# A weight's high and low part written separately, and every instruction held to the planner's order

## The chip, the cores and the metric

The kernel runs on one core of one Trainium2 chip. What counts is the device time of one execution in microseconds (us): the median over several runs. One execution was also recorded by the hardware profiler, and all rows quoted below come from such recordings. The engines are named as in the profile: PE (TensorE, the matrix engine; PEld is its weight load), DVE (VectorE), ACT (ScalarE), POOL (GpSimd) and SP (SyncE, which here only issues transfers).

## The reference, cut to what matters

A decoder trunk of two layers on 256 tokens of 1024 features, all in float32. Each layer has three sub-layers, each with an RMS norm before and after it:

```python
for l in range(DEPTH):
    f = swiglu(rms_norm(x, ffn1_pre_g[l]), ffn1_w_gu[l], ffn1_w_down[l])
    x = x + 0.5 * rms_norm(f, ffn1_post_g[l])
    m = hybrid_mixer(rms_norm(x, mix_pre_g[l]), mix_w_in[l], mix_w_out[l], ...)
    x = x + rms_norm(m, mix_post_g[l])
    f = swiglu(rms_norm(x, ffn2_pre_g[l]), ffn2_w_gu[l], ffn2_w_down[l])
    x = x + 0.5 * rms_norm(f, ffn2_post_g[l])
```

`swiglu` is `silu(x @ gate) * (x @ up)` (2816 wide) times `w_down`. The mixer projects to 2566 columns, runs three heads side by side (a gated linear recurrence, a state-space block in chunks, a gated product over chunks of 128 tokens) and projects back. The weights are 170 MB and each is read once.

## The kernel before, in words

**Matmuls in three parts.** PE multiplies in a rounded format (float32r). To keep float32 precision each operand is split into a high part (a rounded copy) and a low part (what the rounding left), and a product is the sum of three: high x high, high x low, low x high. For a weight, ACT makes the high part (line 406, or line 410 when a norm's gain is multiplied in) and DVE the low part from the original and the high part (line 407 or 411). So each low part waits for its high part on another engine. The normalised input nT is split in the same way: ACT casts the transposed tile, DVE subtracts (both through the helper at line 137).

**Weights.** `weight_units` lists 656 units of 128 rows by up to 512 columns in the order of their use. `weight_chunks` packs them four to a transfer (the first five transfers hold 1, 1, 2, 2 and 2). SP loads a chunk into one of three staging tiles (`dma_chunk`, line 355); the split parts go into one of 17 weight slots, or in some phases into scratch tiles. `fill` (line 374) splits as many units ahead as slots allow.

**Three matmul loops.** In the first block of a feed-forward layer and the first part of the mixer the 128 tokens of each half t are the stationary operand (`a_step`, `mm3`, line 435). In the other feed-forward blocks the weight is stationary, and the high and low part of all 256 tokens pass in one matmul of 512 columns, then one of 256 (`wide_tile`, line 741). The mixer's other columns use `b_tile` (line 718). The product with `w_down` again uses `mm3`: it finishes token half 0 first and has the last four or five steps of half 1 run while half 0 is normalised (`down`, `post`, `pre`).

**Side work.** All that isn't a main matmul is written as a Python generator, a `Chain`: `post` (square sums on ACT, a power on POOL, the update of x on DVE), `pre` (transposes of x on PE, the split into nT, square sums, the power `rs` on POOL, its spread by PE into `rb`), `evac_block` (silu, the product with up, transposes on PE, the split), and the mixer's heads.

**What sets the order.** The kernel carries a model of its own: `self.T` holds a clock for each engine and for transfers, and each operation adds its cost in us (a 512-column matmul 512 x 0.000417 = 0.2135; a high part 0.095 + 512 x 0.000833, and 0.095 more with a gain; a POOL power 0.47). PE's clock is "now". `Chain.op` (line 129) writes an operation when now comes within 0.7 us of the time at which its inputs are ready (PE: not before they are ready; an operation that follows one on its own engine: 2 us). `fill` writes a weight's split when a slot is free, its transfer is modelled as landed and the clocks of DVE and ACT are at most 0.6 us (FILL) ahead of now; the high and the low part are then written one right behind the other (`split_next`, line 393).

**What holds that order.** `keep` (line 294) pins an instruction behind the one written before it on its engine, but only while now is below PIN, 15 modelled us, or when asked for one operation. What is not pinned may be put elsewhere in its engine's queue by the compiler's scheduler, by estimates of its own, as far as data allow. Each engine has one list of instructions, called its queue below.

Of the kernel before, what the change touches and what calls it, by code (L numbers as in the profile page):

```python
# [8 lines left out]
F32 = mybir.dt.float32  # L9
# [3 lines left out]
ALU = mybir.AluOpType  # L13
PSUM = bass.MemoryType.PSUM

P = 128
# [12 lines left out]
HOP = 0.13  # L29
# [4 lines left out]
EXTRA_MIX = (2, 4)  # L34
NF = 3
FIRST = 0
PIN = 15.0

C_GATE, C_REC, C_Z, C_XBC, C_DT, C_UV = 0, 384, 768, 1152, 2048, 2054
XS0, B0, C0 = C_XBC, C_XBC + 384, C_XBC + 640  # L40
# [10 lines left out]
def weight_units():  # L51
    units = []

    def add(name, l, blocks, scale=None):
        units.append((name, l, blocks, scale))

    def ffn(l, w):
        gu, dn, pg = f"ffn{w}_w_gu", f"ffn{w}_w_down", f"ffn{w}"
        for b in range(5):
            for off in (0, DFF):  # L60
                for k in range(KT):
                    add(gu, l, [(k * P, off + b * 512, 512)], (pg, k))
        for k in range(KT):
            add(gu, l, [(k * P, 2560, 256), (k * P, DFF + 2560, 256)], (pg, k))
        for k in range(DKT):
            for n in range(2):
                add(dn, l, [(k * P, n * 512, 512)])

    for l in range(DEPTH):
        ffn(l, 1)  # L70
        for k in range(KT):
            add("mix_w_in", l, [(k * P, C_DT, 6), (k * P, C_Z, 384)], ("mix", k))
        for k in range(KT):
            add("mix_w_in", l, [(k * P, C_UV, 512)], ("mix", k))
        for grp in FGROUPS:
            for k in range(KT):
                add("mix_w_in", l, [(k * P, c, P) for _, _, c in grp], ("mix", k))
        for k in OUT_KTS:
            for n in range(2):
                add("mix_w_out", l, [(k * P, n * 512, 512)], ("norm", k - 3) if 3 <= k < 6 else None)  # L80
        ffn(l, 2)
    return units


def weight_chunks(units):
    chunks, i = [], 0
    head = [1, 1, 2, 2, 2]
    while i < len(units):
        n = head.pop(0) if head else CHUNK
        chunks.append(list(range(i, min(i + n, len(units)))))  # L90
        i += n
    return chunks


def unit_width(u):
    return sum(w for _, _, w in u[2])
# [13 lines left out]
class Chain:  # L110


    def __init__(self, k, t=None):
        self.k = k
        self.t = k.T["pe"] if t is None else t
        self.eng = None
        self.pin = False
# [104 lines left out]
class Kernel:  # L222
    def __init__(self, ctx, tc, x, wts, pf, pb, gpost, wst, wri, out):
        self.tc, self.nc = tc, tc.nc
        self.x_d, self.w_d, self.pf_d, self.pb_d = x, wts, pf, pb
        self.gp_d, self.wst_d, self.wri_d, self.out_d = gpost, wst, wri, out
        mk = lambda n, **k: ctx.enter_context(tc.tile_pool(name=n, **k))
        self.cp = mk("cp", bufs=1)
        self.lp = mk("lp", bufs=1)
        self.sp = mk("sp", bufs=8)  # L230
        self.stg = mk("stg", bufs=NSTG)
        self.scr = mk("scr", bufs=1)
        self.tp = mk("tp", bufs=1)
        self.acc = mk("acc", bufs=1, space=PSUM)
        self.free_slots = {"a": [f"a{i}" for i in range(NSCR)], "m": [f"m{i}" for i in range(8)],
                           "w": [f"w{i}" for i in range(NSLOT)], "f": [f"f{i}" for i in range(NF)]}
        self.banks = [(f"acc{i}", 0.0) for i in range(8)]
        self.side_banks = 0
        self.T = {"pe": 0.0, "act": 0.0, "dve": 0.0, "pool": 0.0, "dma": 2.0}
        self.table = self.last_table = None  # L240
        self.ready = {}
        self.chains = []
        self.units = weight_units()
        self.chunks = weight_chunks(self.units)
        self.u2c = {}
        off = 0
        self.coff, self.cw = [], []
        for ci, c in enumerate(self.chunks):
            o = 0
            for u in c:  # L250
                self.u2c[u] = (ci, o)
                o += unit_width(self.units[u])
            self.coff.append(off)
            self.cw.append(o)
            off += o * P
        self.ctile, self.carrive = {}, {}
        self.next_dma = self.next_split = 0
        self.wt, self.wh, self.wready, self.slot_time = {}, {}, {}, {}
        self.extra, self.keep_free = 0, 4
        self.pairs = {}  # L260


# [31 lines left out]
    def keep(self, ins, pin=False):  # L294
        if pin or self.now() < PIN:
            self.tc.keep_in_program_order(ins)
# [52 lines left out]
    def dma_chunk(self):  # L349
        ci = self.next_dma  # L350
        self.next_dma += 1
        w = self.cw[ci]
        t = self.stg.tile([P, CHUNK * 512], F32, tag="stg", name="stg")
        src = self.w_d[self.coff[ci]: self.coff[ci] + P * w].rearrange("(p n) -> p n", p=P)
        self.nc.sync.dma_start(out=t[:, :w], in_=src)
        self.ctile[ci] = t
        self.T["dma"] = max(self.T["dma"], self.now() + 1.1) + w * P * 4 / 360e3
        self.carrive[ci] = self.T["dma"] + 0.95

    def slot_kind(self):  # L360
# [6 lines left out]
    def fill_time(self):  # L367
        d = self.next_split
        ci, _ = self.u2c[d]
        if self.slot_kind() is None:  # L370
            return 0.0
        return max(self.T["dve"] - FILL, self.T["act"] - FILL, self.carrive.get(ci, 0.0) - 0.3)

    def fill(self):
        did = False
        while self.next_split < len(self.units):
            d = self.next_split
            ci, _ = self.u2c[d]
            while self.next_dma <= min(ci + NSTG - 1, len(self.chunks) - 1):
                self.dma_chunk()  # L380
            kind = self.slot_kind()
            if kind is None:
                break
            lead = d - self.cur
            if self.fill_time() > self.now() and (lead > 2 or self.carrive[ci] > self.now() + 0.3):
                break
            if kind == "a":
                self.extra -= 1
            self.split_next(kind)
            did = True  # L390
        return did

    def split_next(self, kind):
        d = self.next_split
        nc, T = self.nc, self.T
        u = self.units[d]
        w = unit_width(u)
        ci, o = self.u2c[d]
        src = self.ctile[ci][:, o:o + w]
        t, h = self.get([P, 2, 512], F32R, kind)  # L400
        hi, lo = t[:, 0, :w], t[:, 1, :w]
        sc = u[3] is not None
        T["act"] = max(T["act"], self.carrive[ci], self.slot_time.get(h, 0.0) + HOP) + 0.095 + w * 0.000833 + 0.095 * sc
        T["dve"] = max(T["dve"], T["act"] + HOP) + 0.07 + 0.06 * sc + w * 0.00104
        if not sc:
            self.keep(nc.scalar.copy(hi, src))  # L406
            self.keep(nc.vector.tensor_tensor(out=lo, in0=src, in1=hi.bitcast(F32), op=ALU.subtract))  # L407
        else:
            s = self.pcol(u[1], u[3][0], u[3][1])
            self.keep(nc.scalar.activation(hi, src, AF.Copy, scale=s))  # L410
            self.keep(nc.vector.scalar_tensor_tensor(out=lo, in0=src, scalar=s, in1=hi.bitcast(F32),  # L411
                                                     op0=ALU.mult, op1=ALU.subtract))
        self.wt[d], self.wh[d], self.wready[d] = t, h, T["dve"]
        self.next_split += 1

    def unit(self, d):
        self.cur = max(self.cur, d)
# [767 lines left out]
    def build(self):  # L1185
        self.rs, self.ev = [None, None], [None, None]
        self.setup()
        for t in range(2):
            self.add(self.pre(t, ("ffn", 0, 0), [Chain(self, (3.5, 8.9)[q] + (1.7, 0.8)[q] * t) for q in range(2)]))
        self.add(self.layer_params(0))  # L1190
        d = 0
        self.phase = 0
        for l in range(DEPTH):
            for sub in range(3):
                ph = self.phase = self.cur_phase = 3 * l + sub
                nxt = "out" if ph == 3 * DEPTH - 1 else (("ffn", "mix", "ffn")[(sub + 1) % 3], (ph + 1) // 3, ph + 1)
                if sub == 1:
                    d = self.mixer(l, d, nxt)
                else:
                    if sub == 2 and l + 1 < DEPTH:  # L1200
                        self.add(self.layer_params(l + 1))
                    d = self.ffn(l, 1 if sub == 0 else 2, d, nxt)
        self.drain()
# [61 lines left out]
```

## Time and profile before

| | us |
|---|---|
| median of 3 runs | 968.19 (967.71 to 969.85) |
| the profiled execution | 967.81 |
| its span, first to last instruction | 965.8 |
| PE busy | 946.5 (98%) |
| DVE busy | 700.2 (73%) |
| ACT busy | 623.5 (65%) |
| POOL busy | 39.0 (4%) |

How to read the rows below. In a timeline a row gives the start, the time from the first start to the last end of a merged group, the engine, the line, the operation and tiles (out <- in), the count, and in brackets how long the engine had stood idle and what ended that. In a table of stretches a row gives the stretch, its length, the busy time and count of each engine, the clock that PE was granted (1.00 is full speed), the share of the transfer engines that was busy and GB/s. In a table of groups the columns are the busy time of all, the mean in nanoseconds of one, and the idle time before them. A matmul's listed length includes its way through the array; the next one starts earlier.

### The profile page before, as it was taken

Reading aid. Unit: us, or ns where it says so; the run is one execution under the profiler, and the core shown is the slowest. Engines: PE = TensorE matmul, PEld = TensorE weight load, DVE = VectorE, ACT = ScalarE, POOL = GpSimd, SP = SyncE. Lnnn points to the kernel's source line nnn. Section 1 sums busy time; section 2 is a strip of 40 time slices with the busy share of each in tenths; the row PEclk is TensorE's granted clock in tenths of the full one; section 3 lists DMA queues with packets and bytes.
Section 4 is the critical chain, followed back from the end, with each engine's and each line's share of the span. In section 5 each row is a group of like instructions: output and inputs, shape, how many; then the busy total and the mean of one; then the engine's idle time right before and its main releaser. Section 6 shows DMA issues by size and latency. Waiting matters only on the chain.

```text
span 965.8 us, 13918 instructions
## 1 busy us (share of the span) xinstructions
PE 946.5 (98%) x5150; PEld 815.5 (84%) x5150; DVE 700.2 (73%) x1313; ACT 623.5 (65%) x1199; POOL 39.0 (4%) x58
## 2 busy tenths in 40 slices
PE   8899999999999999999999999999999999999997
PEld 6788888889987888888888888888999778888885
DVE  5788876566899877776566788766578997787732
ACT  7687665466967776665465666556589686665631
POOL 1000000011001100000010000000010110000000
PEclk9999999999999999999999999999999999999999
DMA  7745556534225845556526555653531566455611
GB/s 276 302 174 182 203 196 238 185 108 177 88 93 216 316 169 180 198 207 231 187 97 230 175 174 191 245 203 116 195 121 45 204 238 234 141 205 186 221 78 43
DMA packets 27140, 175.51 MB, mean 182 GB/s; under 512 B 3008, under 2 KB 3392, under 8 KB 8384
## 3 DMA queue, kind: packets, MB, share of 16 engines
q1 hardware_dynamic: 25200, 169.93, 49.6%
q10 hardware_dynamic: 1872, 4.70, 1.4%
q8 instruction: 40, 0.66, 0.3%
q14 instruction: 28, 0.23, 0.1%
HBM read 173.57 MB, written 1.05 MB: 181 GB/s over the span
## 4 chain that ended last, share of the span: by engine, by line
PE 85%; DVE 6%; ACT 5%; DMA 2%; issue 1%; POOL 1%; SPq 0%; DVEq 0%; ACTq 0%; POOLq 0%
PE acc L741 41%; PE acc L435 37%; PE acc L137 3%; DVE s_a L137 3%; PE acc L718 3%; DMA stg<-in_wts_dram 2%; ACT s_a L137 2%; DVE s_w L411 1%; ACT s_w L410 1%; ACT L137 1%; ACT junk L137 1%; DVE x L137 1%; DVE s_f L137 1%; POOL postr L137 1%; DVE nT L137 0%
## 5 line engine op out<-in xcount | busy, mean ns | idle before, releaser
L741 PE MATMUL acc<-nT,s_w 128*128 128x512 f32 (+1 forms) x2216 | 392.3, 337 | 0.0
L741 PEld LDWEIGHTS acc<-nT,s_w 128*128 128x128 f32 x2216 | 340.0, 188 | 47.7
L411 DVE SCALAR_TENSOR_TENSOR s_w<-stg,pf,s_w 128x512 fp32r<-128x512 f32 (+2 forms) x436 | 303.8, 732 | 62.9 <-ACT s_w L410 62.3
L410 ACT ACTIVATE s_w<-stg,pf 128x512 fp32r<-128x512 f32 (+2 forms) x436 | 282.1, 702 | 58.7 <-PE acc L435 28.4
L435 PE MATMUL acc<-s_w,s_a 128*128 128x512 f32 x984 | 227.4, 390 | 0.0
L435 PEld LDWEIGHTS acc<-s_w,s_a 128*128 128x128 f32 x984 | 184.4, 188 | 38.1
L407 DVE TENSOR_TENSOR s_w<-stg,s_w 128x512 fp32r<-128x512 f32 x184 | 121.9, 686 | 42.5 <-ACT s_w L406 42.3
L406 ACT CAST s_w<-stg 128x512 fp32r<-128x512 f32 x184 | 107.6, 619 | 52.7 <-PE acc L435 34.3
L435 PE MATMUL acc<-s_w,nT 128*128 128x512 f32 (+1 forms) x522 | 128.6, 393 | 0.6 <-DVE s_w L411 0.3
L137 DVE TENSOR_TENSOR s_m<-acc,s_m 128x256 f32<-128x256 f32 (+2 forms) x172 | 71.3, 417 | 66.2 <-ACT s_m L137 62.2
L435 PEld LDWEIGHTS acc<-s_w,nT 128*128 128x128 f32 x522 | 95.6, 189 | 20.7 <-DVE nT L137 1.8
L137 ACT COPY s_m<-acc 128x256 f32<-128x256 f32 x144 | 52.4, 364 | 89.3 <-PE acc L741 89.3
L718 PE MATMUL acc<-nT,s_w 128*128 128x256 f32 x588 | 75.9, 282 | 0.0
L718 PEld LDWEIGHTS acc<-nT,s_w 128*128 128x128 f32 x588 | 71.5, 188 | 0.3
L435 PE MATMUL acc<-s_w,s_m 128*128 128x512 f32 x192 | 48.4, 399 | 0.1
L137 DVE TENSOR_TENSOR s_f<-acc,gp 128x512 f32<-128x512 f32 x24 | 16.5, 688 | 34.1 <-ACT junk L137 34.0
L435 PEld LDWEIGHTS acc<-s_w,s_m 128*128 128x128 f32 x192 | 34.8, 188 | 7.0 <-DVE s_w L407 0.6
L137 POOL TENSOR_TENSOR postr<-postv,mhalf 128x1 f32<-128x1 f32 x12 | 10.9, 906 | 707.6 <-DVE postv L137 696.4
L137 ACT ACTIVATE junk<-acc 128x512 bf16<-128x512 f32 x24 | 14.2, 593 | 37.7 <-PE acc L435 37.4
L137 ACT CAST s_a<-s_m 128x512 fp32r<-128x512 f32 x36 | 22.2, 618 | 20.6 <-DVE s_m L137 20.6
L137 ACT ACTIVATE s_m<-s_m 128x512 f32<-128x512 f32 x36 | 22.6, 629 | 19.6 <-DVE s_m L137 19.6
L137 DVE TENSOR_TENSOR s_a<-s_m,s_a 128x512 fp32r<-128x512 f32 x36 | 24.7, 687 | 10.3 <-ACT s_a L137 10.3
(138 smaller groups left out, 625.8 us busy)
## 6 DMA issues: line engine op xcount, KB each, us to landing
stg<-in_wts_dram SPq DMA_DIRECT2D x146, 1024.0 KB, 4.8
stg<-in_wts_dram SPq DMA_DIRECT2D x12, 768.0 KB, 4.3
stg<-in_wts_dram SPq DMA_DIRECT2D x4, 780.0 KB, 4.3
gp<-in_gpost_dram ACTq DMA_DIRECT2D x6, 512.0 KB, 5.2
stg<-in_wts_dram SPq DMA_DIRECT2D x3, 512.0 KB, 4.4
x<-in_x_dram SPq DMA_DIRECT2D x4, 256.0 KB, 4.8
out_dram<-x SPq DMA_DIRECT2D x4, 256.0 KB, 2.0
pb<-in_pb_dram ACTq DMA_DIRECT2D x2, 265.0 KB, 5.9
```

The source lines that it names most:

```text
L137: ins = fn(*args, **kw)
L406: self.keep(nc.scalar.copy(hi, src))
L407: self.keep(nc.vector.tensor_tensor(out=lo, in0=src, in1=hi.bitcast(F32), op=ALU.subtract))
L410: self.keep(nc.scalar.activation(hi, src, AF.Copy, scale=s))
L411: self.keep(nc.vector.scalar_tensor_tensor(out=lo, in0=src, scalar=s, in1=hi.bitcast(F32), op0=ALU.mult, op1=ALU.subtract))
L435: self.keep(mm(out, a, b, start=start and i == 0, stop=stop and i == 2))
L718: self.keep(self.nc.tensor.matmul(out, a, b, start=k == 0 and i == 0, stop=k == KT - 1 and i == 2))
L741: self.keep(self.nc.tensor.matmul(out, a, x, start=k == 0 and i == 0, stop=k == KT - 1 and i == 1))
```

## The change

1. `split_next` writes the high part at once as before, but the low part is a chain of its own (`split_low`): it is written when now comes within 0.7 us of the end of its high part, and the unit counts as there only then. At most three such low parts are open at a time.
2. PIN becomes 1e9: everything on ACT, DVE, PE and POOL that goes through `keep` stays in the order in which it was written, to the end. SP's transfers are not pinned, before or after.
3. In the model a transfer starts no earlier than 1.1 us after DVE's clock (whose low part frees the staging tile), and moves 320 GB/s instead of 360.
4. The first two units are split only once the first half of nT for token half 0 (unit 0) or 1 (unit 1) has been written. At the start, the second halves of x are transposed from 9.5 and 10.1 modelled us on instead of 8.9 and 9.7.

```diff
-PIN = 15.0
+RATE = 320e3
+PIN = 1e9
...
+        self.lows = 0
...
-        self.T["dma"] = max(self.T["dma"], self.now() + 1.1) + w * P * 4 / 360e3
+        self.T["dma"] = max(self.T["dma"], self.now() + 1.1, self.T["dve"] + 1.1) + w * P * 4 / RATE
...
-        if self.slot_kind() is None:
+        if self.slot_kind() is None or self.lows > 2 or d < 2 and ("nT", 0, d, 0) not in self.ready:
             return 0.0
...
-            if kind is None:
+            if kind is None or self.lows > 2 or d < 2 and ("nT", 0, d, 0) not in self.ready:
                 break
...
-        T["dve"] = max(T["dve"], T["act"] + HOP) + 0.07 + 0.06 * sc + w * 0.00104
+        c = Chain(self, T["act"])
+        c.eng = "act"
         if not sc:
             self.keep(nc.scalar.copy(hi, src))
-            self.keep(nc.vector.tensor_tensor(out=lo, in0=src, in1=hi.bitcast(F32), op=ALU.subtract))
+            low = c.tt(w, lo, src, hi.bitcast(F32), ALU.subtract)
         else:
             s = self.pcol(u[1], u[3][0], u[3][1])
             self.keep(nc.scalar.activation(hi, src, AF.Copy, scale=s))
-            self.keep(nc.vector.scalar_tensor_tensor(out=lo, in0=src, scalar=s, in1=hi.bitcast(F32),
-                                                     op0=ALU.mult, op1=ALU.subtract))
-        self.wt[d], self.wh[d], self.wready[d] = t, h, T["dve"]
+            low = c.stt(w, lo, src, s, hi.bitcast(F32), ALU.mult, ALU.subtract)
+        self.add(self.split_low(c, low, d, t, h))
         self.next_split += 1
+
+    def split_low(self, c, low, d, t, h):
+
+        self.lows += 1
+        yield from low
+        self.lows -= 1
+        self.wt[d], self.wh[d], self.wready[d] = t, h, c.t
...
-            self.add(self.pre(t, ("ffn", 0, 0), [Chain(self, (3.5, 8.9)[q] + (1.7, 0.8)[q] * t) for q in range(2)]))
+            self.add(self.pre(t, ("ffn", 0, 0), [Chain(self, (3.5, 9.5)[q] + (1.7, 0.6)[q] * t) for q in range(2)]))
```

## The prediction

> **What bounds the kernel now.** I read the page's totals first, then a table of busy time by stretch (the windows view), with the stretches cut where TensorE first stops.
>
> ```profile
> span 965.8 us, 13918 instructions
> PE 946.5 (98%) x5150; PEld 815.5 (84%) x5150; DVE 700.2 (73%) x1313; ACT 623.5 (65%) x1199; POOL 39.0 (4%) x58
> ```
>
> TensorE (PE) is busy for 946.5 of 965.8 us. An edit that only moves instructions cannot win more than the 19.3 us of its idle time and whatever a slow clock costs. The table says where these are (the columns after the stretch: its length, then busy us and instruction count of PE, PEld, DVE, ACT and POOL, then the granted clock, DMA share and GB/s):
>
> ```profile
> 0.00:12.00 12.00, 9.29 (x35) 6.74 (x36) 4.96 (x8) 6.18 (x10) 1.17 (x10) 0.86 0.78 270
> 35.90:42.20 6.30, 3.31 (x15) 2.90 (x14) 6.25 (x11) 4.77 (x10) 0.00 (x0) 0.73 0.82 313
> 42.20:196.00 153.80, 153.80 (x807) 132.01 (x807) 112.38 (x203) 98.48 (x181) 0.90 (x1) 1.00 0.55 195
> 196.00:203.00 7.00, 6.54 (x37) 5.67 (x36) 6.41 (x11) 6.19 (x15) 0.95 (x2) 1.00 0.17 46
> 243.00:304.00 61.00, 58.53 (x368) 51.29 (x368) 55.41 (x127) 49.35 (x108) 3.77 (x4) 1.00 0.35 121
> 304.00:481.00 177.00, 176.99 (x922) 150.97 (x921) 130.57 (x233) 112.88 (x207) 6.15 (x8) 1.00 0.60 215
> 481.00:484.00 3.00, 2.54 (x16) 1.92 (x15) 2.70 (x5) 2.18 (x6) 0.27 (x1) 1.00 0.00 0
> 669.00:672.00 3.00, 2.53 (x17) 1.88 (x15) 2.73 (x5) 2.69 (x7) 0.24 (x1) 1.00 0.02 5
> 717.00:780.00 63.00, 60.20 (x375) 52.26 (x375) 56.91 (x131) 50.93 (x111) 4.48 (x5) 1.00 0.36 124
> 780.00:965.80 185.80, 178.88 (x926) 152.45 (x924) 122.33 (x204) 100.51 (x187) 2.09 (x3) 0.99 0.48 171
> ```
>
> Length less PE's busy time gives the idle time: 2.71 us at the start, 2.99 around 39 us, 0.46 at 196, 2.47 in the first mixer's second half and the boundary behind it, 0.46 at 481, 0.47 at 669, 2.80 in the second mixer, 6.92 in the last stretch, which is the tail after the last matmul. Together 19.28 of the 19.3 us. In the two long feed-forward stretches shown PE does not stop at all (153.80 of 153.80, 176.99 of 177.00): there nothing can be won, and something could be lost.
>
> The clock column is below 1 in two places. I cut them finer:
>
> ```profile
> 4.64:8.05 3.41, 2.38 (x10) 1.23 (x9) 1.73 (x3) 2.52 (x4) 0.00 (x0) 1.00 0.90 332
> 8.05:11.46 3.41, 3.18 (x12) 2.09 (x11) 2.46 (x5) 1.92 (x3) 0.00 (x0) 0.50 0.93 308
> 35.36:38.77 3.41, 1.00 (x6) 0.59 (x4) 2.82 (x5) 3.41 (x7) 0.00 (x0) 1.00 0.96 293
> 38.77:42.18 3.41, 2.83 (x12) 2.74 (x13) 3.41 (x7) 1.88 (x4) 0.00 (x0) 0.50 0.85 324
> 243.00:246.40 3.40, 2.30 (x20) 2.13 (x20) 3.40 (x10) 3.28 (x7) 0.00 (x0) 1.00 0.26 43
> ```
>
> After a thin 3.41 us (1.00 busy) the clock is halved for the next 3.41 us, though PE has work again: 2.83 us of work at half speed, 1.41 us lost. The start has the same thing at 8.05 to 11.46 (3.18 us of work, up to 1.59 us lost).
>
> **The stop at 36 us (term one).** The timeline around it:
>
> ```profile
> 32.75 1.28 ACT L137 ACT_TABLE_LOAD   x1
> 34.63 0.68 ACT L137 ACTIVATE s_m<-acc,rs 128x512 f32<-128x512 f32 x1
> 35.20 3.17 ACT L410 ACTIVATE s_w<-stg,pf 128x512 fp32r<-128x512 f32 x5
> 35.95 2.74 DVE L411 SCALAR_TENSOR_TENSOR s_w<-stg,pf,s_w 128x512 fp32r<-128x512 f32 x4 [1.41 <-ACT s_w L410]
> 38.61 1.28 DVE L137 TENSOR_TENSOR s_m<-acc,s_m 128x512 f32<-128x512 f32 x2
> 39.35 1.97 PE L137 MATMUL acc<-ident,s_m 128*128 128x128 f32 x8 [2.99 <-DVE s_m L137]
> ```
>
> These are the first block's two silu results (s_m, ACT) and the two products gate times up (DVE, L137) that PE must transpose. The second silu ends at 34.63 + 0.68 = 35.31; the products start only at 38.61. In between DVE runs four low parts (L411), the first of which itself waited 1.41 us for its high part. DVE was idle when the products could have run, and stood behind lows whose inputs were not there. PE, whose queue holds the transposes next, waits 2.99 us.
>
> Whose order is this? By the planner's code, not the planner's: the fill of weights stops while the modelled ACT time is over 0.6 us ahead of PE's, and the table load and two silus push it 2.6 us ahead; the first product is issued once its silu is less than 0.7 us away. At most one low comes between the products. Beyond 15 modelled us, though, nothing is pinned (PIN), and the compiler's scheduler, by its own estimates, put four lows in front. With PIN at 1e9 the written order holds on all engines. With lows as chain steps, a low is written when due rather than beside its high part, so the pinned DVE queue does not stand 0.6 us behind each high part.
>
> In the new order the first product can run at 34.04 + about 0.7 for its silu, so from 34.75, and both are done by 36.1. PE came to the transposes at 39.35 - 2.99 = 36.36, so the wait goes whole. Its 2.99 us and the 1.41 us of half clock behind it: **-4.4 us**. What would be late next are the transposes' casts on ACT, but PE has matmuls of the next block then. The four lows come after the products; 17 weight slots are ahead of PE there, which is the cover; without it each late low would cost its 0.7 us.
>
> [...]
>
> **The start (term two).** Times of the first weights (L410 high, L411 low) and of the activations' halves (nT):
>
> ```profile
> 4.93 0.58 ACT L137 CAST nT<-acc 128x512 fp32r<-128x512 f32 x1 [2.16 <-PE acc L137]
> 5.41 0.73 ACT L410 ACTIVATE s_w<-stg,pf 128x512 fp32r<-128x512 f32 x1
> 6.17 0.75 DVE L411 SCALAR_TENSOR_TENSOR s_w<-stg,pf,s_w 128x512 fp32r<-128x512 f32 x1 [4.26 <-ACT s_w L410]
> 6.19 0.50 PE L435 MATMUL acc<-s_w,nT 128*128 128x512 f32 x1
> 6.84 0.68 DVE L137 TENSOR_TENSOR nT<-acc,nT 128x512 fp32r<-128x512 f32 x1
> 6.91 0.72 ACT L410 ACTIVATE s_w<-stg,pf 128x512 fp32r<-128x512 f32 x1
> 6.98 1.87 PE L435 MATMUL acc<-s_w,nT 128*128 128x512 f32 x4 [0.28 <-DVE s_w L411]
> 8.30 1.34 ACT L410 ACTIVATE s_w<-stg,pf 128x512 fp32r<-128x512 f32 x2 [0.67 <-DMA stg<-in_wts_dram]
> 8.34 0.68 DVE L137 TENSOR_TENSOR nT<-acc,nT 128x512 fp32r<-128x512 f32 x1
> 9.08 0.80 PE L435 MATMUL acc<-s_w,nT 128*128 128x512 f32 x1 [0.23 <-DVE nT L137]
> ```
>
> DVE takes the first weight's low (6.17 to 6.92) before the first nT low (6.84 to 7.52), though the latter's input is there at 4.93 + 0.58 = 5.51. The new condition (the first two weights wait until their half of nT is written) reverses the two: nT low about 5.55 to 6.23, weight low 6.2 to 6.95, second nT low 6.9 to 7.6, second weight low from the end of its high part (6.91 + 0.72 = 7.63) to 8.4. ACT's order stays. PE has done five matmuls when the sixth starts at 9.08, right after the second nT low (8.34 + 0.68 = 9.02). With everything of units 0 and 1 there by 8.4, it will have done ten. A 512-wide matmul in a row takes (7.99 - 0.40)/33 = 0.230 us:
>
> ```profile
> 289.77 7.99 PE L435 MATMUL acc<-s_w,s_m 128*128 128x512 f32 x34
> ```
>
> (0.40 is the last one's own length, the mean of L435's s_m group.) Five of them: **-1.1 us**. Units 2 and 3 still end ACT's wait for their transfer at 8.30, so no more than that is sure. Bounds: if the fuller stretch 4.64 to 8.05 keeps the clock at 1.00, another 1.6 goes, to -2.7. Against that, the second halves' transposes are written from 9.5 modelled us on, not 8.9: +0.6 if PE needs them at once. I take no clock gain: 2.38 of 3.41 busy was followed by the half clock here, 2.30 of 3.40 at 243 was not, so these rows give no threshold.
>
> **Boundaries and mixers (term three).** Their idle time is 0.46 + 2.47 + 0.46 + 0.47 + 2.80 = 6.66 us, PE waiting in its queue for transposes. The planner writes a PE side operation only when its inputs are ready by its own costs. For ACT and DVE these agree with the trace (five high parts in 3.17 us, the last of them 0.72: (3.17 - 0.72)/4 = 0.61 each; the code has 0.617). Two do not:
>
> ```profile
> L137 POOL TENSOR_TENSOR postr<-postv,mhalf 128x1 f32<-128x1 f32 x12 | 10.9, 906 | 707.6 <-DVE postv L137 696.4 <-DVE vx L137 11.1
> L137 POOL TENSOR_TENSOR rs<-vx,mhalf 128x1 f32<-128x1 f32 x12 | 8.5, 705 | 42.3 <-DVE vx L137 40.6 <-PE acc L137 1.7
> ```
>
> The code gives POOL 0.47 us for these: 0.44 and 0.24 too little. It gives a 512-wide matmul 0.2135 where the trace has 0.230, which errs the other way: a chain of 2.6 modelled us passes 12 matmuls, and PE comes to the transposes 12 x 0.0165 = 0.2 us later than modelled. So of a late POOL result 0.24 and 0.04 us are left: 10 boundary chains x 0.24 + 12 x 0.04 = 2.9 us of new waits. I take half of the old 6.66 away, since the part that comes from lows in front of due work goes and the part from dependent chains stays: -3.3 + 2.9, so **-0.4 us**; bounds -5 (three quarters go, nothing new) and +8 (the rival below).
>
> The transfer model (320e3, and the wait for DVE) changes no transfer: SP's queue holds the same loads with the same waits on freed staging tiles. It only moves high parts later in ACT's written order, and so work behind them earlier; a transfer later than modelled would now hold ACT's queue. Zero, covered by the 17 slots; no more than three lows are open, so a tile comes free at most some 2 us (three lows of 0.7) later. The tail of 6.92 us is one dependent chain: zero.
>
> **Sum.** -4.4 - 1.1 - 0.4 = -5.9. The profiled execution took 967.81 us (span 965.8 and 2.0 around it), which gives 961.9; the median of the runs, 968.19, is 0.4 higher: **962.3 us**. A measurement of this kernel tells 0.2%, 1.9 us, from no change.
>
> **Rivals.** *Slower: PE's pinned queue.* PE can no longer take matmuls in front of a late transpose or of the rs product. Its place is the twelve post chains and twelve rs chains; its price is POOL's whole error, 12 x 0.44 + 12 x 0.24 = 8.2 us, plus one stretch of half clock in each mixer (2 x 1.4) where waits add up: 11 - 5.5 = +5.5, **973.7 us**. It decides once a chain costs over 5.5/24 = 0.23 us more than now. For it: every wait of PE in the table is of this kind. Against: matmuls are modelled too short, which gives PE slack. [...]
>
> *No change: the order at 36 us is the planner's own,* so that pinning keeps it. Then -1.1 - 0.4 = -1.5 is left, **966.7 us**; the same comes out if term one is had but comes back as small waits in the long stretches (4.4 us are 1.3% of the 331 us of the two shown). For it: one profile cannot show who ordered those lows. Against: the planner's conditions above.
>
> *More: all lows in front of due work go,* the start keeps its clock and three quarters of 6.66 go: -4.4 - 2.7 - 5.0 = -12.1, **956.1 us**. For it: at 243 and 297 DVE is nearly full (55.41 of 61.00) and order matters most. Against: the POOL rows.
>
> **Chances.** Forecast 0.50 (959 to 966), more 0.20, no change 0.16, slower 0.14. So faster 0.70, within 0.2% 0.16, slower 0.14. The range runs from 956.0, the larger gain, to 970.0, leaving most of the slower case out above and a little below.
>
> **What would show it.** In the changed profile: PE busy without a stop from 35.9 to 42.2 and clock 1.00 there, the products straight after the silus; the first nT low ahead of the first L411; ten matmuls by about 9.1. Boundary waits of 0.3 to 0.6 us remain, now for both token halves. It is wrong if PE stops in the long feed-forward stretches, if transposes wait for POOL by over 0.5 us, or if ACT waits for transfers with evacuations behind them.

## The result: 3.6% slower, and the profile after

The changed kernel takes 1003.7 us (median of 4 runs, 1002.05 to 1004.05), the kernel before 968.2. The ratio is 1.0361, 95% interval 1.0345 to 1.0378. The prediction was 962.3 us, faster; it was wrong in sign and size. The profiled execution after took 1002.05 us. Its page begins:

```profile
span 1000.3 us, 13877 instructions
PE 963.4 (96%) x5150; PEld 823.3 (82%) x5150; DVE 717.4 (72%) x1313; ACT 625.5 (63%) x1199; POOL 36.1 (4%) x58
```

PE's idle time went from 19.3 to 1000.3 - 963.4 = 36.9 us. To see where, I cut the span where PE stops (columns as before: length, busy us and count of PE, PEld, DVE, ACT, POOL, granted clock, DMA share, GB/s):

```profile
36.03:42.20 6.17, 4.45 (x29) 4.02 (x29) 5.70 (x11) 4.17 (x8) 0.00 (x0) 1.00 0.55 191
49.30:85.00 35.70, 32.26 (x166) 26.32 (x165) 26.57 (x59) 23.03 (x43) 0.00 (x0) 0.95 0.45 162
262.00:281.00 19.00, 13.96 (x79) 12.62 (x79) 16.54 (x38) 12.97 (x28) 0.00 (x0) 0.73 0.32 111
745.00:805.00 60.00, 52.60 (x302) 45.34 (x301) 49.11 (x109) 41.28 (x92) 2.46 (x3) 0.91 0.35 124
```

The stop at 36 us is shorter (1.72 us idle instead of 2.99, the clock stays at 1.00). New stops stand at 49 to 85 us, where PE never stopped before (behind them, from 85 to 198, it again never stops), and in both mixers, 7.4 us in 745 to 805. At 262 to 281 and 745 to 805 the clock is low too (0.73 and 0.91). What PE waits for has changed. The rows for weights (total us, times, longest; 19.4 us together):

```profile
PE acc L727 <- DVE s_w L138: 6.8, 4, 2.3
PE acc L750 <- DVE s_w L138: 4.2, 5, 1.3
PE acc L727 <- ACT s_w L413: 3.3, 4, 0.9
PE acc L444 <- DVE s_w L138: 3.1, 8, 0.5
PE acc L444 <- ACT s_w L413: 2.0, 2, 1.0
```

s_w are the split weights. Before, PE waited 0.3 us for them in the whole kernel. (Line 138 is now the helper's, for lows too; 413 the high part, 444, 727 and 750 the three matmul loops.)

A second measure serves for all runs below. There are 4752 main matmuls, the first being number 0. The start of numbers 120, 936, 1440, 3312, 3816 and 4751 in the one trace, less the same start in the trace of before, says what the six stages cost, for one execution of each kernel. Before, they end at 42.4 (start and first block), 200.2 (first feed-forward), 299.8 (mixer), 673.4 (two feed-forwards), 773.3 (mixer) and 958.5 us (feed-forward). Us lost against before in each:

```
                                   start  ff     mixer  2 ff   mixer  ff     sum
after                              -3.7    7.3   13.3    4.2   12.9    0.5   34.5
e1  before, all pinned             -3.3    9.6   13.7    7.6   13.7    1.5   42.9
e2  after, nothing pinned          -1.4    1.5    0.8    0.9    0.4    0.8    3.0
e3  weights free, rest pinned      -1.6    0.1   12.5    1.2   13.3    1.0   26.6
e5  only PE pinned                  0.9    0.1    5.4    0.3    4.5    0.4   11.6
e7  all but PE pinned              -4.3    1.3    8.7    2.2    8.0    1.5   17.3
e14 only ACT pinned                -3.7    1.3    7.3    2.8    8.3    1.9   17.8
e15 only DVE pinned                -0.2    0.4    9.3    1.3    7.8    1.3   19.8
e6  FILL 2.0                       -6.4    2.5   14.4   -0.4   14.5   -0.4   24.2
e13 FILL 2.0, all but PE pinned    -6.4    1.2   12.5   -0.2   11.7   -0.1   18.7
e8  mixers not pinned              -1.9    7.9    1.4    5.1    1.3    1.4   15.2
e9  FILL 2.0, mixers not pinned    -6.4    0.9    0.9    0.0    0.5    0.4   -3.6
e10 e9 with POOL's price at 0.95   -6.3    0.8    2.0    6.2    1.6    3.7    8.0
e11 after, old transfer model      -1.9    6.3   13.2    5.0   13.0    0.3   36.0
e12 before, new start              -1.1    0.0    0.1    0.0    1.1    1.3    1.3
e16 pins up to 45 us, FILL 2.0     -6.6    2.0    0.8    1.0    0.8    2.2    0.2
```

**How PE runs out of weights.** By main matmul 1260 (257.9 us before, 262.0 after) PE has begun the last tile of the mixer's third column group, which uses units 164 to 171, and the next tile needs units 172 to 179. The high parts done by then (the row gives the stretch and its length, then busy us and count of one line's instructions, then clock, DMA share and GB/s), lines 410 and 406 before:

```profile
0.00:257.90 257.90, 86.54 (x136) 0.99 0.56 199
0.00:257.90 257.90, 26.21 (x45) 0.99 0.56 199
```

lines 413 and 409 after:

```profile
0.00:262.00 262.00, 83.49 (x130) 0.99 0.53 188
0.00:262.00 262.00, 25.07 (x44) 0.99 0.53 188
```

136 + 45 = 181 against 130 + 44 = 174. Counting from unit 0, before has all of units 172 to 179 and one more, after only 172 and 173. A stock of two is what the planner writes when ACT and DVE are full: `fill` then goes on only while `lead`, the distance from the unit in use to the one to be split, is at most 2. That line is the same in both kernels, so the nine units of before are the compiler's scheduler's doing. ACT's queue shows how they came. Before:

```profile
242.08 3.13 ACT L410 ACTIVATE s_w<-stg,pf 128x384 fp32r<-128x384 f32 x6
245.12 0.60 ACT L406 CAST s_w<-stg 128x512 fp32r<-128x512 f32 x1
```

After, with PE's own rows behind ACT's:

```profile
247.01 1.72 ACT L413 ACTIVATE s_w<-stg,pf 128x512 fp32r<-128x512 f32 x3
252.85 1.34 ACT L138 ACTIVATE s_a<-acc,pf 128x256 f32<-128x256 f32 x3 [2.81 <-PE acc L138]
262.67 1.28 ACT L138 ACT_TABLE_LOAD   x1
264.59 1.61 ACT L413 ACTIVATE s_w<-stg,pf 128x384 fp32r<-128x384 f32 x3
```

```profile
254.73 9.58 PE L727 MATMUL acc<-nT,s_w 128*128 128x256 f32 x80
265.25 0.50 PE L727 MATMUL acc<-nT,s_w 128*128 128x256 f32 x2 [0.94 <-ACT s_w L413]
267.92 2.31 PE L727 MATMUL acc<-nT,s_w 128*128 128x256 f32 x7 [2.18 <-DVE s_w L138]
271.04 0.80 PE L727 MATMUL acc<-nT,s_w 128*128 128x256 f32 x2 [0.80 <-ACT s_w L413]
```

Before, seven high parts ran at 242 to 245.7, ahead of the recurrence's sigmoids. After, ACT stood idle for 2.81 us for PE and made no high part from 248.7 to 264.6, since the sigmoids, tanhs and table loads were written first and the queue was pinned. Then PE stops at each new weight: it waits for ACT (high), for DVE (low), for ACT again.

### The profile page after: what moved, and what is told of

It is laid out like the page before. It is cut to its first block, busy times and chain, and to the rows that moved or that the text cites. A ratio compares the mean times of both kernels' runs of the same rounds, so it can differ in the third digit from the quotient of the medians.

```text
span 1000.3 us, 13877 instructions
## 1 busy us (share of the span) xinstructions
PE 963.4 (96%) x5150; PEld 823.3 (82%) x5150; DVE 717.4 (72%) x1313; ACT 625.5 (63%) x1199; POOL 36.1 (4%) x58
## 4 chain that ended last, share of the span: by engine, by line
PE 85%; DVE 7%; ACT 3%; DMA 2%; issue 1%; POOL 1%; SPq 0%; POOLq 0%; DVEq 0%; ACTq 0%
PE acc L750 39%; PE acc L444 35%; PE acc L727 6%; PE acc L138 5%; DVE s_w L138 3%; DVE s_a L138 2%; DMA stg<-in_wts_dram 2%; ACT s_w L413 2%; ACT junk L138 1%; DVE s_f L138 1%; DVE s_m L138 1%; DVE x L138 0%; POOL postr L138 0%; POOL s_a L138 0%; ACT s_m L138 0%
## 5 line engine op out<-in xcount | busy, mean ns | idle before, releaser
L138 DVE TENSOR_TENSOR s_w<-stg,s_w 128x512 fp32r<-128x512 f32 x184 | 119.5, 688 | 40.0 <-ACT s_w L409 39.1
L727 PE MATMUL acc<-nT,s_w 128*128 128x256 f32 x588 | 79.8, 293 | 10.1 <-DVE s_w L138 6.8
L727 PEld LDWEIGHTS acc<-nT,s_w 128*128 128x128 f32 x588 | 75.0, 198 | 12.9 <-DVE s_w L138 8.3
L444 PE MATMUL acc<-s_w,s_m 128*128 128x512 f32 x192 | 53.8, 417 | 4.8 <-DVE s_w L138 2.5
L444 PEld LDWEIGHTS acc<-s_w,s_m 128*128 128x128 f32 x192 | 35.9, 195 | 14.5 <-DVE s_w L138 4.5
```

Source lines behind the costliest of these rows:

```text
L138: ins = fn(*args, **kw)
L444: self.keep(mm(out, a, b, start=start and i == 0, stop=stop and i == 2))
L727: self.keep(self.nc.tensor.matmul(out, a, b, start=k == 0 and i == 0, stop=k == KT - 1 and i == 2))
```

## The experiments

Three explanations were told apart. Late weights (theory one in the expectations): the pinned queues hold the splits behind side work, where the planner wrote them. PE's pinned queue (theory two): PE stands in front of late side work. Parts of the change other than the pins: separate lows, transfer model, limit of open lows. Of the last, the limit never binds: with 99 in its place the program built is the same.

**e1, the pins alone.** The kernel before with

```diff
-PIN = 15.0
+PIN = 1e9
```

> The kernel before with only PIN set to 1e9: high and low stay side by side, the transfer model stays. Late weights (the pinned queues hold every split behind side work, where the planner wrote it, so that PE runs out of split weights): slower than before, 1000 to 1025 us, and at least as slow as the change, since each low now also stands ahead of due DVE work while its high part runs; PE waits for weights in both mixers. Separate lows or the transfer model to blame: within 5 us of before, 963 to 973. PE's pinned queue (transposes late behind POOL) to blame: 990 to 1010, but PE's waits end on side work (x, s_a, s_m), not on weights.

Measured: 1015.84 us, 1.0494 times before (1.0462 to 1.0526). As late weights had it, and slower than the change. PE waits:

```profile
PE acc L741 <- DVE s_w L411: 10.2, 10, 1.3
PE acc L718 <- DVE s_w L411: 7.9, 10, 1.6
PE acc L137 <- DVE s_a L137: 6.3, 7, 1.5
```

So the pins cause the loss, and the change's separate lows and other edits win back a fifth to a quarter of it (34.5 against 42.9 us in the table, whose execution of e1 is the fastest of four; 35.5 against 48.2 by the medians).

**e2, the change without pins beyond 15 us.**

```diff
-PIN = 1e9
+PIN = 15.0
```

> The change with PIN back at 15: separate lows, the transfer model and the new start stay, the compiler's scheduler orders the rest as before. Late weights, and also PE's pinned queue: the loss is gone, 962 to 972 us, and the start keeps its gain of about 1 us. Separate lows or the transfer model to blame: the loss stays, 985 us or more.

Measured: 970.64 us, 1.0029 (1.0016 to 1.0042). The loss is gone. What remains of the change costs 0.3%: the 1.4 us that the start is ahead are given back in the first feed-forward layer, and the rest comes in small pieces.

**e3, weights free, the rest pinned.** Each side instruction is pinned behind the last side instruction of its engine; high and low parts aren't pinned.

```diff
-            self.keep(nc.scalar.copy(hi, src))
+            self.keep_w(nc.scalar.copy(hi, src))
...
+    def keep_w(self, ins):
+        if self.now() < PIN_W:
+            self.keep(ins)
```

> The change with one thing freed: the high and low parts of weights aren't pinned beyond 15 modelled us, while all other instructions keep their written order among themselves. Late weights: the splits can move ahead of side work again, PE's waits for weights go, and the time falls by over two thirds of the loss, to 960 to 978 us. PE's pinned queue: nothing of the loss goes, 997 us or more, since PE's queue and all side work are as in the change.

Measured: 995.14 us, 1.0298 (1.0278 to 1.0317). Between the two expectations, so neither theory is whole. The feed-forward layers lose nothing any more (0.1 and 1.2 us in the table): there late weights are all. The mixers lose as much as before, but PE now waits for side work:

```profile
PE acc L140 <- ACT s_a L140: 12.8, 8, 2.4
PE acc L140 <- POOL s_a L140: 5.5, 4, 2.0
PE acc L762 <- DVE s_w L140: 0.4, 1, 0.4
```

**e6, everything pinned, splits written earlier.**

```diff
-FILL = 0.6
+FILL = 2.0
```

> The change with one constant altered, FILL 2.0 for 0.6: all is still pinned, but the planner writes a split as long as the modelled clocks of ACT and DVE are at most 2.0 us ahead of PE's, so splits stand earlier in the queues, ahead of side work. Late weights: most of the loss goes with the order still pinned, 955 to 975 us; PE's waits for weights in the mixers nearly vanish, waits for side work stay or grow a little. PE's pinned queue: 1000 us or more, side work gets later still.

Measured: 992.08 us, 1.0254 (1.0239 to 1.027). A third of the loss went, and the time lies between the two theories' numbers. Again the feed-forward layers are nearly healed (2.5, -0.4, -0.4) and the start is 6.4 us ahead of before, while the mixers lose 14.4 and 14.5. Waits for weights are gone from PE's list; now the splits hold up side work. The rows of ACT, DVE and PE at the end of the first mixer:

```profile
286.21 2.56 ACT L413 ACTIVATE s_w<-stg,pf 128x512 fp32r<-128x512 f32 x4 [2.69 <-DMA stg<-in_wts_dram]
288.67 0.51 ACT L138 ACTIVATE junk<-s_a 128x384 bf16<-128x384 f32 x1
```

```profile
286.53 4.71 DVE L138 SCALAR_TENSOR_TENSOR s_w<-stg,pf,s_w 128x512 fp32r<-128x512 f32 x7
291.17 0.14 DVE L138 TENSOR_SCALAR ynv<-yss 128x1 f32<-128x1 f32 x1
```

```profile
285.64 1.45 PE L138 MATMUL acc<-s_a,s_a 128*128 128x64 f32 x12
295.36 0.87 PE L138 MATMUL acc<-ident,s_a 128*128 128x128 f32 x3 [8.27 <-DVE s_a L138]
```

A pinned high part waits 2.69 us for its transfer with the state-space head's norm (junk) behind it on ACT; seven lows stand ahead of that norm on DVE; PE's transposes of it come 8.27 us late.

**e5 and e7, PE pinned alone, and all but PE.** `keep` asks for the engine:

```diff
-        if pin or self.now() < PIN:
+        if pin or self.now() < 15.0 or ins.ins.engine == mybir.EngineType.PE:
```

> The change with only PE's queue pinned beyond 15 modelled us; ACT, DVE and POOL are ordered by the compiler's scheduler. Rigid order of splits and side work on ACT and DVE (theory one: the loss needs these two queues pinned): nearly all of the loss goes, 964 to 975 us. PE's pinned queue alone (theory two, the rival of the prediction): the mixers still lose most of what they lose now, 985 us or more, with PE waiting for side work.

> The reverse: ACT, DVE and POOL pinned as in the change, PE's queue free beyond 15 us. Theory one: splits are as late as in the change and no matmul can run without its weight, so most of the loss stays, 990 to 1004 us. Theory two: PE passes late transposes and the loss goes, 975 us or less.

(e7 has 15.0 as PE's limit and PIN for the other engines.) Measured: e5 978.22 us, 1.0108 (1.0084 to 1.0132); e7 985.51 us, 1.0188 (1.0165 to 1.0211). Both between their two expectations. PE's queue costs 1.1% by itself, most of it in the mixers, with PE waiting 7.4 us for side work on ACT; a single wait of 2.8 us for a weight takes the gain of the start. The other three engines' queues (e7) cost 1.9% with PE free. Weights are only a part of that: 5.0 us of waits for them in the mixers' loop, and 8.5 us for x at the borders between layers (3.2 before, 5.3 in e2). e7's rows:

```profile
PE acc L727 <- DVE s_w L138: 5.0, 4, 1.6
PE acc L138 <- DVE x L138: 8.5, 5, 3.5
```

In the feed-forward layers e7 loses little (1.3 and 2.2 us), where the change loses 7.3 and 4.2.

**e8 and e9, no pins in the mixers,** and e9 with FILL 2.0 outside them:

```diff
-        if pin or self.now() < PIN:
+        if pin or self.now() < PIN and not self.free:
...
+        self.free = True
         gp = self.load_gpost(l * 3 + 1)
...
+        fill = FILL if self.free else 2.0
+        return max(self.T["dve"] - fill, self.T["act"] - fill, self.carrive.get(ci, 0.0) - 0.3)
```

(The last two lines are e9's alone; `free` ends with the mixer.)

> The change with nothing pinned while a mixer is written (from its start to the end of its output product); feed-forward layers stay pinned. Theory one, by stage: the mixers' losses of some 13 and 14 us go, the first feed-forward layer's 7 us and smaller ones stay: 968 to 980 us. If the mixers' loss comes from weights already short before the mixer starts, it stays: 990 us or more.

> As the one without pins in the mixers, and in the feed-forward layers FILL is 2.0, so that splits are written further ahead there. Theory one: no stage loses; what is left is the gain at the start and at the first block's transposes, some 4 us: 961 to 967 us, faster than the kernel before. If early splits harm feed-forward layers or the borders to the mixers: 970 us or more.

Measured: e8 982.76 us, 1.0157 (1.0133 to 1.0181), 3 us above its range; e9 965.05 us, 0.9975 (0.9963 to 0.9987). The mixers' loss comes from the pins in the mixers (13 to 1.4 us), the feed-forwards' from splits written too late there (7.9 and 5.1 in e8, 0.9 and 0.0 in e9). e9 beats the kernel before by a quarter of a per cent. Its rows around the first block show what the prediction's first term was about:

```profile
35.29 1.27 ACT L138 ACTIVATE s_m<-acc,rs 128x512 f32<-128x512 f32 x2
36.06 1.28 DVE L138 TENSOR_TENSOR s_m<-acc,s_m 128x512 f32<-128x512 f32 x2
36.98 0.60 PE L138 MATMUL acc<-ident,s_m 128*128 128x128 f32 x4
```

The products follow the silus at once, PE doesn't wait, and the clock stays at 1.00: the first stage is 6.4 us shorter than before.

**e10, a higher price for POOL's powers.** e9 with `c.op("pool", 0.95, ...)` for the powers instead of 0.47.

> The last one (FILL 2.0 and pins in feed-forward layers, none in the mixers, 965 us) with the planner's price of POOL's powers set to 0.95 instead of 0.47, so that the written order puts PE's transposes behind the power's real length. If a price set too low makes PE stand in its pinned queue (the prediction's slower rival): PE's waits for x, 5.4 us, fall by half or more and the time by 1 to 3 us, to 962 to 964. If these waits come from the scheduled stretches or from DVE being busy: within 1.5 us of 965.

Measured: 975.58 us, 1.0076 (1.0061 to 1.0091), slower than e9 by some 10 us, which neither expectation had. PE's waits for x are 5.6 us in 2 waits instead of 5.4 in 5, so they don't fall, and 2.6 us of waits for nT are new; the loss is at the borders behind both mixers (6.2 and 3.7 us in the table). There a wait of 2.8 us for x and one of 1.3 us for nT now stand close together, and half clock follows:

```profile
296.13:302.95 6.82, 5.44 (x16) 3.82 (x16) 6.82 (x12) 3.00 (x6) 0.99 (x1) 0.50 0.50 171
```

The granted clock of the profiled execution is 0.990, in e9's 0.996. The price wasn't truer for all powers: in the trace of after those for rs take 547 to 553 ns, those for postr 547 to 989. A higher price for these steps didn't make the written order better; why the waits bunch there stays open.

**e11, the old transfer model in the change.**

```diff
-        self.T["dma"] = max(self.T["dma"], self.now() + 1.1, self.T["dve"] + 1.1) + w * P * 4 / RATE
+        self.T["dma"] = max(self.T["dma"], self.now() + 1.1) + w * P * 4 / 360e3
```

> The change with the old transfer model (360 GB/s, no wait for DVE's clock), all else as in the change. Theory one has no part for the transfer model: 998 to 1010 us, near the change's 1003.7. If pessimistic modelled transfers are what writes splits late: under 990 us.

Measured: 1004.66 us, 1.0381 (1.0361 to 1.0402), the change's time. The transfer model has no part in the loss.

**e12, the start alone.** The kernel before with the condition on the first two units and the times 9.5 and 0.6, nothing else.

> The kernel before with the start's part alone: the first two weights wait for their half of nT, and the second halves of x come from 9.5 and 10.1 modelled us; low parts beside high parts, PIN 15. By the prediction's second term the first nT low precedes the first weight low, about ten main matmuls are done by 9.1 us rather than five, and 1 us is won: 965.5 to 968. If the transfers of units 2 and 3 bind at once: no gain, 968 to 970.

Measured: 963.99 us (961.61 to 968.93), 0.9949 (0.9929 to 0.9969). More than forecast. The profiled execution is the slowest of the four, 968.93 us; it has the nT low first on DVE and is 1.1 us ahead at the end of the first stage, though PE is idle for 1.7 of the 15 us from 30 to 45 and the clock is 0.89 there. The other three executions have no trace, but their mean granted clock is on record: 0.998 to 0.999, against 0.995 in the profiled one. That is up to 0.004 x 967 = 3.9 us of full speed, so less half clock can be half or more of what they win beyond it; in which stretches stays open. e9 contains this start, and the two intervals touch; which of them is the faster isn't settled.

**e13, FILL 2.0 with PE free.** e6 with PE's queue free beyond 15 us.

> FILL 2.0 with ACT, DVE and POOL pinned throughout and PE's queue free beyond 15 us. In the mixers all of it pinned lost some 30 us in two waits of 8 us and others on side work behind splits. If PE's rigid queue turns late side work into those waits: most goes, 966 to 975 us. If the output product needs that late side work as its input anyway, so that nothing can be passed: 980 us or more.

Measured: 986.71 us, 1.0191 (1.0176 to 1.0207). The long waits stay, as the second expectation had it: the output product needs that side work as its input, so PE has nothing to put in its place. PE's two waits for s_a from DVE come to 19.0 us (16.8 in e6), the longer is 9.5.

**e14 and e15, only ACT or only DVE pinned.**

> The change with only ACT's queue pinned beyond 15 modelled us. If late high parts on ACT carry the loss (a low can't precede its high, and ACT's queue holds the highs behind side work): most of what is lost with PE free stays, 980 to 990 us, PE waits for weights. If the lows on DVE carry it: 975 us or less.

> The change with only DVE's queue pinned beyond 15 us. If ACT's queue carries the loss: 975 us or less, as highs run early and only wait for their lows. If DVE's queue carries it: 980 to 990 us, since a matmul needs the low too and the lows keep their late place in DVE's queue.

Measured: e14 983.8 us, 1.0164 (1.015 to 1.0178); e15 988.91 us, 1.0213 (1.0193 to 1.0234). Each queue by itself is enough for a loss of this size. It isn't weights alone: a matmul needs both parts, and PE waits 4.0 us in e14 and 5.2 us in e15 for them, but 8.5 and 6.6 us for x (5.3 in e2). The losses don't add up (both and POOL's together, e7, cost 1.9%).

**e16, pins up to 45 modelled us, with FILL 2.0 there and 0.6 behind.**

> The change with PIN at 45 instead of 1e9 and FILL 2.0 up to there, 0.6 behind: the written order holds for the start and the first block's transposes and nothing after. If all gains of the change lie there and all its losses behind: 961 to 965 us, with some 4 to 6 us won by 43 us of the profile and no more than 2 us lost later. If the order pinned at the start costs later stretches: 967 us or more.

Measured: 966.13 us (11 runs), 0.9977 (0.9968 to 0.9986). The gain of the start stands by itself (6.6 us in the table), but most of it is given back in small pieces (2.0, 0.8, 1.0, 0.8, 2.2).

## Why the prediction was wrong, point by point

**What bounds the kernel** was read rightly: PE, with nothing to win in the long feed-forward stretches and "something could be lost". It was lost there and in the mixers.

**The failing step** is in the third term: "Zero, covered by the 17 slots". It was said of high parts that come later in ACT's written order, and term one leans on the same cover ("17 weight slots are ahead of PE there"). Slots were counted, not what stands in them: the written order keeps two units in stock where ACT and DVE are full, and PE's waits for weights went from 0.3 to 19.4 us. It isn't the transfer model that moves the splits (e11). The trace of before could have warned: at matmul 1260, 181 high parts were done, nine beyond the 172 used or in use, in a stretch where DVE was busy for 55.41 of 61 us. And the working used one rule of the planner for one side alone. It said that "the fill of weights stops while the modelled ACT time is over 0.6 us ahead", to show that few lows stand ahead of due products. The same rule writes the splits behind side work whenever ACT or DVE is full and two units are in stock. In the kernel before the compiler's scheduler undid this by moving splits ahead; the pins forbid it. Without those pins the time is 970.64 us (e2), with them alone 1015.84 (e1).

**Term one** (-4.4 us at 36 us): the order there was half read. Before, four high parts stood between a wait for a transfer and the table load:

```profile
30.16 2.57 ACT L410 ACTIVATE s_w<-stg,pf 128x512 fp32r<-128x512 f32 x4 [3.37 <-DMA stg<-in_wts_dram]
```

The text took the first silu at its old time, 34.04. In the written order seven stand there (30.07 and 33.37), so the silus come later (36.00). PE's transposes start 1.6 us earlier than before (37.75 and 39.35), and PE still waits 1.72 us; a wait of the same kind, 1.6 us, is new in the second feed-forward layer. After:

```profile
30.07 3.39 ACT L413 ACTIVATE s_w<-stg,pf 128x512 fp32r<-128x512 f32 x5 [0.90 <-DMA stg<-in_wts_dram]
33.37 1.32 ACT L413 ACTIVATE s_w<-stg,pf 128x512 fp32r<-128x512 f32 x2
34.71 1.28 ACT L138 ACT_TABLE_LOAD   x1
36.00 1.27 ACT L138 ACTIVATE s_m<-acc,rs 128x512 f32<-128x512 f32 x2
37.75 0.66 PE L138 MATMUL acc<-ident,s_m 128*128 128x128 f32 x4 [1.72 <-DVE s_m L138]
```

The stage is 3.7 us shorter, 1.2 of it by main matmul 60 (24.4 and 23.3 us), so 2.5 belong to this term: right mechanism, size 2.5 instead of 4.4. It is 1.3 us of the wait and the half clock's 1.4. With FILL 2.0 it gives more (e6, e9).

**Term two** (-1.1 us at the start) held in mechanism. DVE takes the nT low first (5.66), then the weight's:

```profile
5.66 0.69 DVE L138 TENSOR_TENSOR nT<-acc,nT 128x512 fp32r<-128x512 f32 x1 [3.74 <-ACT nT L138]
6.28 0.75 DVE L138 SCALAR_TENSOR_TENSOR s_w<-stg,pf,s_w 128x512 fp32r<-128x512 f32 x1
7.09 3.49 PE L444 MATMUL acc<-s_w,nT 128*128 128x512 f32 x13 [0.29 <-DVE s_w L138]
```

Nine main matmuls have started by 9.1 us, six before; ten were forecast. The clock stays at 1.00 from 5.18 to 63.20 in this execution, the bound that wasn't taken. The gain isn't all the order's. At main matmul 30 the change is 2.0 us ahead of before, and e1, which has the old start and the clock at 1.00 there too, 0.9. So some 1.0 us are the order's (1.1 forecast) and 0.9 the clock's, which another execution may not have; 0.8 are given back by matmul 60.

**Term three's boundaries and mixers.** PE's waits for side work there (for x and s_a, 6.66 us before) were to be 6.3. The list of after has 1.4 us for x, 2.1 for s_a from POOL and 0.2 for rs, 3.7 in all. POOL's powers for rs, whose price the term held to be 0.24 us too low (their mean before was 705 ns), took 547 to 553 ns. So the term was too cautious; the loss came from what it left out.

**The slower rival** was forecast at 973.7 us with a chance of 0.14 and named PE's queue behind POOL's power. PE's queue has a part (e5, 1.1%), but it waits for side work on ACT, and a higher price for POOL's powers made the order worse (e10, with the mixers unpinned). The rival that came true, weights late in ACT's and DVE's queues, stood in the text only as a sign: "if PE stops in the long feed-forward stretches".

**The half clock** was counted rightly as a price of a stop, but not for the new stops:

```profile
63.20:66.62 3.42, 3.24 (x10) 2.76 (x11) 3.04 (x6) 2.20 (x5) 0.00 (x0) 0.50 0.91 331
268.00:278.25 10.25, 8.32 (x34) 7.39 (x35) 10.02 (x23) 6.31 (x16) 0.00 (x0) 0.50 0.59 200
305.55:308.96 3.41, 3.41 (x8) 2.72 (x9) 2.87 (x6) 2.61 (x6) 0.00 (x0) 0.50 0.68 226
742.46:745.87 3.41, 3.41 (x11) 2.78 (x10) 2.94 (x8) 0.84 (x2) 0.00 (x0) 0.50 0.74 274
759.52:769.76 10.24, 7.34 (x29) 6.46 (x30) 10.02 (x23) 7.28 (x16) 0.00 (x0) 0.50 0.45 158
```

In these five PE works 3.24 + 8.32 + 3.41 + 3.41 + 7.34 = 25.7 us at half speed, so up to 12.9 us are lost beside the waits; before, 3.18 + 2.83 = 6.0 us cost up to 3.0. Of the 34.5 us, 17.6 are PE's added idle time and up to 9.9 the half clock's; some 7 us are left that these rows don't place. The half clock came without a long wait: none of PE's waits for weights is over 2.3 us.

## What to carry to other kernels

Before instructions are pinned in a written order, look in the trace for what the scheduler had moved, above all for work that runs ahead of need: count in the trace how far ahead the stock is where the engines are full. Here a pinned order served only in the first 45 us (6.6 us won by the stage with FILL 2.0, 1.9 us of it left in the whole time, e16). It cost where several chains and a stock share the same queues: there giving the one the front put the other late (e3, e6). Pin a stretch, and check the stretches one by one.

## What the runs showed that was not expected

Pinning only ACT costs 1.64% and only DVE 2.13%, together with POOL 1.88%: here the losses of queues that feed the same consumer didn't add. Half clock came without a stop as long as the 2.99 us of before, after shorter ones in a row (0.39, 0.73 and 0.65 us ahead of 63.20, 0.94 and 2.18 us ahead of 268.00), and the busy share of the 3.41 us ahead of it gives no threshold:

```profile
264.59:268.00 3.41, 0.58 (x3) 0.38 (x3) 3.37 (x8) 3.39 (x7) 0.00 (x0) 1.00 0.00 0
59.79:63.20 3.41, 2.54 (x9) 1.08 (x7) 3.41 (x6) 3.21 (x6) 0.00 (x0) 1.00 0.59 195
35.90:39.31 3.41, 1.69 (x13) 1.50 (x13) 2.97 (x6) 2.48 (x6) 0.00 (x0) 1.00 0.71 251
```

The first two, with 0.58 and 2.54 us of PE busy, were followed by half clock; the third, with 1.69, was not.
